# The last product of the MLP as seven block products (Strassen), with float32 activations

## The chip, the cores and the metric

The kernel runs on one core of a Trainium2 chip. The metric is the device time of one execution in microseconds, as the median of several runs. A separate execution was taken by the hardware profiler; all views of the profile come from that one. Engines are named as in the profile: PE is TensorE, DVE is VectorE, ACT is ScalarE, POOL is GpSimd, SP is SyncE, which here issues the loads and stores.

## The reference

One layer of a streaming encoder on 512 positions of width 1024: four parallel token mixers, a cross-attention, and a gated MLP. All numbers are float32. The change touches the MLP only:

```python
hf = _rms_norm(x, norm_ffn_pre[l])                        # 512 x 1024
u = _dwconv_causal(hf @ w_up[l], ffn_dw[l]) + ffn_dw_b[l] # w_up 1024 x 5632, conv of width 3
u_g, u_v = jnp.split(u, 2, axis=-1)                       # two halves of 2816
yff = (jax.nn.silu(u_g) * u_v) @ w_down[l]                # w_down 2816 x 1024
x = x + _rms_norm(yff, norm_ffn_post[l])                  # the output
```

## The kernel before

Every large product is formed in a split form: each float32 operand x is held as a high part hi (a cast by ACT to the format float32r) and a low part lo = x - hi (a subtraction by DVE, which reads x and hi and rounds to float32r). A product is then three matmuls, hi·hi, hi·lo and lo·hi, into the same PSUM bank (`mm3`). A matmul has a stationary operand of 128x128 and a moving one of 128x512.

`run_blocks` takes a stream of jobs, one for each block of weights, and writes out three jobs ahead: the load (SP), the cast (ACT) and the subtraction (DVE) of a block are written three blocks before the matmuls that use it. A scheduler then orders the instructions of each engine when the program is built, by a cost model; each engine works through its own queue in that order. Weights land in tiles `wr` (two buffers) and are split into `wh` and `wl`, four buffers each.

The MLP has two stages. `up_jobs` forms 44 blocks of the up-projection (24 matmuls each). The two blocks of a row group j (0 to 21) pass the convolution (one ACT operation and two of DVE from PSUM each), the gate (a tanh and two DVE operations, L1291 and L1292), and then `split` (ACT L152, DVE L153) writes the activations of j into `acth` and `actl`, which hold all 22 groups of 128 rows for all 512 positions.

`down_jobs` has 22 jobs, one for each group of 128 rows of `w_down`, with [128, 1024] weights each. For each, the 4 groups of 128 positions and the 2 halves of the output columns give 8 accumulators, which are the 8 banks of PSUM (tags mm, av, sc, tr, two each): 8 x 3 matmuls for a job, 528 in all. The last four jobs are held back, so that the accumulators end one after the other, and each group of positions is normed (square on ACT, L1345; root on POOL, L261 and L264; products and sums on DVE, L1348 and L1355) and stored while PE goes on with the next one.

Of the kernel before, what the change touches and what calls it, by code (L numbers as in the profile page):

```python
# [16 lines left out]
F32 = mybir.dt.float32  # L17
F32R = mybir.dt.float32r
AF = mybir.ActivationFunctionType
ALU = mybir.AluOpType  # L20
# [4 lines left out]
P = 128  # L25
S = 512
D = 1024
NT = S // P
# [5 lines left out]
NF = DFF // P  # L34
EPS = 1e-6
WB = 2 * 520
# [46 lines left out]
def hybrid_layer(ctx: ExitStack, tc: tile.TileContext, a: dict, out: bass.AP):  # L83
    nc = tc.nc
    V, A, G, PE, SP = nc.vector, nc.scalar, nc.gpsimd, nc.tensor, nc.sync


    gp = ctx.enter_context(tc.tile_pool(name="g", bufs=1))
# [7 lines left out]
    def bank(tag=None):  # L96
        if tag is None:
            turn_of.n += 1
            tag = "av" if turn_of.shared and turn_of.n % 2 else "mm"
        return psum.tile([P, 512], F32, tag=tag, name=f"ps_{tag}", bufs=2)  # L100
# [7 lines left out]
    w_up, w_down = a["w_up"][0], a["w_down"][0]  # L108
# [19 lines left out]
    for i in range(8):  # L128
        n = ("wh", "wl")[i % 2]
# [3 lines left out]
        elif i < 6:  # L133
            n = ("fz_raw", "fz", "fe", "fu", "fd")[i - 1]
# [7 lines left out]
    def weights_tile(kind):  # L142

        i = w_used[kind]
        w_used[kind] += 1
        return w_tiles.pop((kind, i), None) or gp.tile([P, WB], F32R, tag=f"{kind}{i % 4}", name=kind)


    def split(ps, hi, lo, scale=None):

        if scale is None:
            A.copy(hi, ps)  # L152
            V.tensor_tensor(lo, ps, hi.bitcast(F32), ALU.subtract)  # L153
        else:
            A.activation(hi, ps, AF.Copy if isinstance(scale, float) else AF.Identity, scale=scale)
            V.scalar_tensor_tensor(lo, ps, scale, hi.bitcast(F32), ALU.mult, ALU.subtract)
# [39 lines left out]
    def run_blocks(jobs, ahead=3):  # L196


        jobs = iter(jobs)
        pending = []  # L200

        def fetch():
            while True:
                job = next(jobs, None)
                if job is None:
                    return
                if job[1] is None:
                    pending.append((job[0] or (), job[2]))
                else:
                    pending.append((load_weights(*job[:2], *job[3:]), job[2]))  # L210
                if job[0] is not None:
                    return

        for _ in range(ahead):
            fetch()
        while pending:
            if pending[0][0]:
                fetch()
            w, body = pending.pop(0)
            body(*w)  # L220
            bg.tick()
# [9 lines left out]
    def mm3(ps, w_hi, w_lo, x_hi, x_lo, first, last):  # L231

        matmul(ps, w_hi, x_hi, first, False)
        matmul(ps, w_hi, x_lo, False, False)
        matmul(ps, w_lo, x_hi, False, last)
# [20 lines left out]
    def rstd_of(pool, parts, n=1):  # L256

        m = pool.tile([P, n], F32, tag="st_m", name="st_m", bufs=4)
        r = pool.tile([P, n], F32, tag="st_r", name="st_r", bufs=4)
        if len(parts) == 2:  # L260
            G.tensor_scalar(m, parts[0], parts[1], EPS, ALU.add, ALU.add)  # L261
        else:
            G.tensor_scalar(m, parts[0], EPS, None, ALU.add)
        G.tensor_tensor(r, m, nhalf[:, :n], ALU.pow)  # L264
        return r
# [21 lines left out]
    def new_ht():  # L287
        if ht_tiles:
            return ht_tiles.pop(0), ht_tiles.pop(0)
        return (gp.tile([P, NK, S], F32R, tag="hth", name="hth"),  # L290
                gp.tile([P, NK, S], F32R, tag="htl", name="htl"))
# [67 lines left out]
    for i, plan in enumerate(plans):  # L359
        r_t = m1p.tile([P, P], F32, tag="fbias" if i == 2 else "ck", name=f"rows{i}", bufs=2)  # L360
        n = 0
# [906 lines left out]
    def open_ffn():  # L1268
        bg.drain("n1")
        close(ns.work_)  # L1270
        close(ns.xp_)
        close(ns.xm_)
        ns.fp_, ns.fp = new_pool("ffn", False)
        ns.work = ns.fp
        ns.act = (ns.fp.tile([P, NF, S], F32R, name="acth"), ns.fp.tile([P, NF, S], F32R, name="actl"))
        ns.post = ns.fp.tile([P, D], F32, name="g_ffn")
        G.dma_start(ns.post, a["norm_ffn_post"][0].partition_broadcast(P))

    def up_jobs():
        st, held = {}, []  # L1280

        def done(j, i, ps):
            if i == 0:
                st[j] = ns.fp.tile([P, 2, S], F32, tag="c", name="c", bufs=2)
            c, ch = st[j], i * NF + j
            A.activation(c[:, i], ps, AF.Identity, bias=pc("fb", ch), scale=pc("fdw2", ch))
            taps(c[:, i], ps, lambda k: pc("fdw01", k * 44 + ch), 3)
            if i == 1:
                th = ns.fp.tile([P, S], F32, tag="th", name="th")
                A.activation(th, c[:, 0], AF.Tanh, scale=0.5)  # L1290
                V.scalar_tensor_tensor(th, th, 1.0, c[:, 0], ALU.add, ALU.mult)  # L1291
                V.scalar_tensor_tensor(c[:, 1], th, 0.5, c[:, 1], ALU.mult, ALU.mult)  # L1292
                split(c[:, 1], ns.act[0][:, j], ns.act[1][:, j])


        for n in range(2 * NF):
            def body(hi, lo, n=n):
                j, i = divmod(n, 2)
                if n > 3:
                    ps = bank()  # L1300
                    channel_major(ps, (hi, lo), ns.hf)
                    done(j, i, ps)
                    return
                if n == 0:
                    bg.drain("n0")
                ps = bank(("mm", "sc")[n % 2])
                (channel_major if n else by_pass)(ps, (hi, lo), ns.hf, slice(0, S // 2))
                held.append((j, i, ps, (hi, lo)))
                if n == 3:
                    open_ffn()  # L1310
                    for j, i, ps, w in held:
                        (channel_major if i or j else by_pass)(ps, w, ns.hf, slice(S // 2, S))
                        done(j, i, ps)
            yield *cols(w_up, n % 2 * DFF + n // 2 * P), body, V, same, HALF_SHIFT if n < 4 else 0

    def down_jobs():
        tail = 4
        held, ps = [], []

        def step(t, i, kk, hi, lo):  # L1320
            sl, csl = slice(t * P, (t + 1) * P), slice(i * 512, (i + 1) * 512)
            mm3(ps[t][i], ns.act[0][:, kk, sl], ns.act[1][:, kk, sl], hi[:, csl], lo[:, csl], kk == 0, kk == NF - 1)

        for kk in range(NF):
            def body(hi, lo, kk=kk):
                if kk == 0:
                    tags = (("mm", "mm"), ("av", "av"), ("sc", "sc"), ("tr", "tr"))
                    ps.extend([bank(n) for n in pair] for pair in tags)
                if kk < NF - tail:
                    for t in range(NT):  # L1330
                        for i in range(2):
                            step(t, i, kk, hi, lo)
                    return
                held.append((kk, hi, lo))
                if kk < NF - 1:
                    return
                for t in range(NT):
                    res, o = ns.out[t], ns.fp.tile([P, 2, S], F32, tag="c", name="o", bufs=2)
                    ms = []
                    for i in range(2):  # L1340
                        for w in held:
                            step(t, i, *w)
                        ms.append(ns.fp.tile([P, 1], F32, tag=f"pm{i}", name=f"pm{i}", bufs=2))
                        junk = ns.fp.tile([P, S], F32, tag="th", name="junk")
                        A.activation(junk, ps[t][i], AF.Square, scale=1.0 / math.sqrt(D), accum_out=ms[i])  # L1345
                        if i == 1:
                            r = rstd_of(ns.fp, ms)
                        V.tensor_tensor(o[:, i], ps[t][i], ns.post[:, i * 512:(i + 1) * 512], ALU.mult)  # L1348
                    for i in range(2):
                        sl = slice(i * 512, (i + 1) * 512)  # L1350
                        parts = 2 if (t, i) == (NT - 1, 1) else 1
                        for q in range(parts):
                            n = 512 // parts
                            c, d = slice(q * n, (q + 1) * n), slice(sl.start + q * n, sl.start + (q + 1) * n)
                            V.scalar_tensor_tensor(o[:, i, c], o[:, i, c], r, res[:, d], ALU.mult, ALU.add)  # L1355
                            SP.dma_start(out[t * P:(t + 1) * P, d], o[:, i, c])
            yield w_down[kk * P:(kk + 1) * P, :], [P, D], body

    def all_jobs():
        yield from mixer_jobs()  # L1360
# [43 lines left out]
```

## Time and profile before

| | |
|---|---|
| runs | 1080.5, 1080.79, 1081.97 us; median 1080.79 us |
| profiled execution | 1081.09 us, of which the span of the profile is 1079.3 us |
| mean granted clock of TensorE | 0.998 |
| PE, weight loads, DVE, ACT, POOL busy | 99%, 84%, 64%, 43%, 10% of the span |
| down stage, first to last matmul | 953.0 to 1073.0 us |

The span runs from the first to the last instruction of the profiled core. The 1.8 us between it and the execution's time lie around the program. Busy shares are means over stages; a stage is read from a table of stretches, and single instructions from the timeline. A line number in the profile is that of the helper that issues the instruction, so groups are told apart by tile names as well.

### The profile page before, as it was taken

Reading aid. Unit: us, or ns where it says so; the run is one execution under the profiler, and the core shown is the slowest. Engines: PE = TensorE matmul, PEld = TensorE weight load, DVE = VectorE, ACT = ScalarE, POOL = GpSimd, SP = SyncE. Lnnn points to the kernel's source line nnn. Section 1 sums busy time; section 2 is a strip of 40 time slices with the busy share of each in tenths; the row PEclk is TensorE's granted clock in tenths of the full one; section 3 lists DMA queues with packets and bytes.
Section 4 is the critical chain, followed back from the end, with each engine's and each line's share of the span. In section 5 each row is a group of like instructions: output and inputs, shape, how many; then the busy total and the mean of one; then the engine's idle time right before and its main releaser. Section 6 shows DMA issues by size and latency. Waiting matters only on the chain.

```text
span 1079.3 us, 14199 instructions
## 1 busy us (share of the span) xinstructions
PE 1071.2 (99%) x5453; PEld 910.7 (84%) x5453; DVE 695.9 (64%) x1131; ACT 465.3 (43%) x785; POOL 104.0 (10%) x189
## 2 busy tenths in 40 slices
PE   9999999999999999999999999999999999999997
PEld 8888888888888988888888899998888888888886
DVE  7899996466666467857464486868666666642224
ACT  5322222467464364654443365645444444431112
POOL 4000001000101033323000120120000000000001
PEclk9999999999999999999999999999999999999999
DMA  6433433332222243233155343134333333333322
GB/s 203 116 98 91 90 107 95 93 98 78 59 81 78 69 127 98 81 96 117 59 176 180 113 146 92 57 99 118 97 98 98 98 98 98 98 98 97 98 78 78
DMA packets 145848, 109.29 MB, mean 101 GB/s; under 512 B 3647, under 2 KB 133292, under 8 KB 145781
## 3 DMA queue, kind: packets, MB, share of 16 engines
q1 hardware_dynamic: 143219, 99.85, 31.1%
q0 software_dynamic: 2560, 8.54, 2.7%
q8 instruction: 43, 0.70, 0.3%
q14 instruction: 24, 0.20, 0.1%
q10 hardware_dynamic: 2, 0.00, 0.0%
HBM read 106.27 MB, written 2.11 MB: 100 GB/s over the span
## 4 chain that ended last, share of the span: by engine, by line
PE 99%; ACT 0%; DVE 0%; POOLq 0%; issue 0%; DVEq 0%; POOL 0%; ACTq 0%
PE ps_mm L224 52%; PE ps_av L224 31%; PE ps_sc L224 8%; PE ps_tr L228 3%; PE ps_tr L224 3%; PE ps_mm L431 1%; PE ps_av L431 1%; PE ps_mm L373 0%; PE ps_sc L378 0%; DVE o L1355 0%; PE ps_tr L415 0%; POOLq L1400 0%; ACT junk L1345 0%; ACT hth L152 0%; ACT hth L421 0%
## 5 line engine op out<-in xcount | busy, mean ns | idle before, releaser
L184 DVE TENSOR_TENSOR wl<-wr,wh 128x1024 fp32r<-128x1024 f32 (+1 forms) x172 | 212.2, 1235 | 194.2 <-ACT wh L183 193.7
L183 ACT CAST wh<-wr 128x1024 fp32r<-128x1024 f32 (+1 forms) x172 | 180.1, 1049 | 318.4 <-PE ps_mm L224 127.8
L224 PE MATMUL ps_mm<-hth,wh 128*128 128x512 f32 (+1 forms) x616 | 231.4, 382 | 0.2 <-ACT hth L152 0.2
L224 PE MATMUL ps_mm<-hth,wl 128*128 128x512 f32 (+1 forms) x616 | 230.0, 380 | 0.0
L224 PE MATMUL ps_mm<-htl,wh 128*128 128x512 f32 (+1 forms) x616 | 229.9, 380 | 0.0
L224 PEld LDWEIGHTS ps_mm<-hth,wh 128*128 128x128 f32 x616 | 114.3, 188 | 21.1 <-ACT hth L152 0.5
L224 PEld LDWEIGHTS ps_mm<-hth,wl 128*128 128x128 f32 x616 | 114.0, 188 | 21.1
L224 PEld LDWEIGHTS ps_mm<-htl,wh 128*128 128x128 f32 x616 | 114.0, 188 | 20.4 <-DVE htl L153 0.2
L224 PE MATMUL ps_av<-hth,wh 128*128 128x512 f32 (+1 forms) x328 | 122.4, 373 | 0.0
L224 PE MATMUL ps_av<-htl,wh 128*128 128x512 f32 (+1 forms) x328 | 122.4, 373 | 0.0
L224 PE MATMUL ps_av<-hth,wl 128*128 128x512 f32 (+1 forms) x328 | 122.3, 373 | 0.0
L584 DVE SCALAR_TENSOR_TENSOR y<-y,par,y 128x499 f32<-128x499 f32 (+28 forms) x120 | 82.3, 729 | 0.2
L224 PEld LDWEIGHTS ps_av<-htl,wh 128*128 128x128 f32 x328 | 61.7, 188 | 10.9
L224 PEld LDWEIGHTS ps_av<-hth,wh 128*128 128x128 f32 x328 | 61.5, 188 | 10.9
L224 PEld LDWEIGHTS ps_av<-hth,wl 128*128 128x128 f32 x328 | 61.5, 188 | 10.8
L224 PE MATMUL ps_mm<-y,wh 128*128 128x512 f32 x192 | 61.2, 394 | 0.0
L261 POOL TENSOR_SCALAR st_m<-pm,pm 128x1 f32<-128x1 f32 x12 | 6.4, 533 | 435.6 <-ACT junk L1345 350.2
L224 PEld LDWEIGHTS ps_mm<-y,wh 128*128 128x128 f32 x192 | 35.4, 188 | 6.8
L152 ACT CAST acth<-c 128x512 fp32r<-128x512 f32 x22 | 13.7, 621 | 56.9 <-DVE c L1292 56.9
L224 PE MATMUL ps_mm<-y,wl 128*128 128x512 f32 x96 | 37.6, 392 | 0.0
L907 POOL TENSOR_SCALAR fbias<-ck,cq 128x128 f32<-128x128 f32 (+3 forms) x32 | 27.6, 868 | 68.0 <-DVE st L913 63.5
L518 DVE SCALAR_TENSOR_TENSOR c<-ps_mm,par,c 128x510 f32<-128x510 f32 (+1 forms) x44 | 32.8, 745 | 0.7
(379 smaller groups left out, 1901.4 us busy)
## 6 DMA issues: line engine op xcount, KB each, us to landing
wr<-in_w_up SPq DMA_DIRECT2D x44, 512.0 KB
wr<-in_w_in SPq DMA_DIRECT2D x38, 512.0 KB
wr<-in_w_gate SPq DMA_DIRECT2D x32, 512.0 KB
wr<-in_w_down SPq DMA_DIRECT2D x22, 512.0 KB
wr<-in_w_branch SPq DMA_DIRECT2D x16, 512.0 KB
wr<-in_w_out SPq DMA_DIRECT2D x8, 512.0 KB
xr<-in_w_xkv SPq DMA_DIRECT2D x8, 512.0 KB
wr<-in_w_in SPq DMA_DIRECT2D x4, 520.0 KB
```

The source lines that it names most:

```text
L152: A.copy(hi, ps)
L183: order(A.copy(hi, raw[:, :n]))
L184: low.tensor_tensor(lo, raw[:, :n], hi.bitcast(F32), ALU.subtract)
L224: PE.matmul(ps, lhs, rhs, start=start, stop=stop)
L228: PE.transpose(ps, x, ident[:n, :n])
L261: G.tensor_scalar(m, parts[0], parts[1], EPS, ALU.add, ALU.add)
L431: keep(PE.matmul(banks[c][:, :S // 2], w[p == 1][:, k, c * P:(c + 1) * P], ht[p == 2][:, i * 4 + k, :S // 2], start=(i, p, k) == (0, 0, 0) ...
L518: V.scalar_tensor_tensor(dst[:, s:], src[:, :S - s], w(k), dst[:, s:], ALU.mult, ALU.add)
L584: V.scalar_tensor_tensor(dst[:, s:], src[:, :S - s], pc("conv_dw", k * 4 + j), dst[:, s:], ALU.mult, ALU.add)
L907: G.tensor_scalar(bias[:, :w], ck[j][:, :w], -1.0, cq[:, qt, head:head + 1], ALU.mult, ALU.add)
```

## The change

The last product is an [512 x 2816] by [2816 x 1024] one. It is cut in 2 x 2 blocks on both sides: positions 0 to 255 and 256 to 511, rows of `w_down` in even and odd groups of 128 (11 pairs), and columns 0 to 511 and 512 to 1023. Instead of the eight block products, seven are formed of sums and differences of the blocks (the variant with 15 sums), each as three matmuls as before: 7 products x 2 groups of 128 positions x 11 pairs x 3.

In the up stage the activations are no longer split. The last DVE operation of the gate writes them as float32 into tiles `qa` (4 blocks of 256 positions for each pair) and `qb` (3 blocks); for each pair POOL then forms four sums of 128x256 (`activation_sums`).

The down stage has two phases over the 11 pairs, with two jobs for each pair. Phase 0 forms M1, M6 (job 0) and M5, M7 (job 1) in all 8 banks; phase 1 forms M2, M3 (job 0) and M4 (job 1) in 6 of them. For a pair, phase 0 loads 768 KB of `w_down` into a tile `dw` (three buffers); POOL forms three sums of 128x512; ACT and DVE split four weight blocks of 512 columns and the four activation blocks (1024 columns in all). Phase 1 loads 512 KB again; POOL forms one sum; ACT and DVE split three weight blocks of 512 and three activation blocks (768 columns). The split activations lie in four slots, made of the two tiles (`hth`, `htl`) that held the input of the up stage; the split weights lie in the old four `wh` and `wl`. Between the phases (`middle`) DVE adds up M1, M6, M5 and M7. At the end (`ends`) the last three pairs of phase 1 are held back, and M4, M3 and M2 are added to what the middle left, normed and stored.

The core of the diff (the loops that end the result are cut, and so is the code that is taken out):

```diff
-        ns.act = (ns.fp.tile([P, NF, S], F32R, name="acth"), ns.fp.tile([P, NF, S], F32R, name="actl"))
+        ns.quart = [(ns.fp.tile([P, 4, S // 2], F32, tag=f"qa{q}", name="qa"),
+                     ns.fp.tile([P, 3, S // 2], F32, tag=f"qb{q}", name="qb")) for q in range(NF // 2)]
...
-                V.scalar_tensor_tensor(c[:, 1], th, 0.5, c[:, 1], ALU.mult, ALU.mult)
-                split(c[:, 1], ns.act[0][:, j], ns.act[1][:, j])
+                x = ns.quart[j // 2]
+                V.scalar_tensor_tensor(x[j % 2][:, 0:2].rearrange("p a b -> p (a b)"), th, 0.5, c[:, 1],
+                                       ALU.mult, ALU.mult)
+                if j % 2:
+                    activation_sums(*x)
...
+    def activation_sums(x, z):
+        G.tensor_tensor(x[:, 2], x[:, 1], z[:, 1], ALU.add)
+        G.tensor_tensor(x[:, 3], x[:, 0], x[:, 1], ALU.subtract)
+        G.tensor_tensor(x[:, 1], x[:, 2], x[:, 0], ALU.subtract)
+        G.tensor_tensor(z[:, 2], z[:, 0], x[:, 1], ALU.subtract)
...
+        pairs, hold, half = NF // 2, 3, S
+        order = [(phase, q) for phase in range(2) for q in range(pairs)]
...
+        def load(n):
+            while len(raws) < min(n, len(order)):
+                phase, q = order[len(raws)]
+                raw = ns.fp.tile([P, 3 * half], F32, tag="dw", name="dw", bufs=3)
+                rows = slice((2 * q + phase) * P, (2 * q + phase + 1) * P)
+                SP.dma_start(raw[:, :D], w_down[rows, :])
+                if phase == 0:
+                    SP.dma_start(raw[:, D:], w_down[(2 * q + 1) * P:(2 * q + 2) * P, half:])
+                raws.append(raw)
+
+        def split_to(hi, lo, x):
+            A.copy(hi, x)
+            V.tensor_tensor(lo, x, hi.bitcast(F32), ALU.subtract)
+
+        def activations(phase, q):
...
+                slot = parts["slots"][(phase * pairs + q - 1) % 4]
...
+            split_to(hi, lo, ns.quart[q][phase].rearrange("p a b -> p (a b)"))
...
+        def weights(phase, q, job):
+            if job == 0:
+                load(phase * pairs + q + 3)
+                activations(phase, q)
+            raw = raws[phase * pairs + q]
+            b = [raw[:, i * half:(i + 1) * half] for i in range(3)]
+            if (phase, job) == (1, 1):
+                G.tensor_tensor(b[2], b[0], t2.pop(q), ALU.subtract)
...
+                split_to(*both, b[2])
+                return [both],
+            hi, lo = weights_tile("wh"), weights_tile("wl")
+            both = [(hi[:, i * half:(i + 1) * half], lo[:, i * half:(i + 1) * half]) for i in range(2)]
+            if (phase, job) == (0, 0):
+                G.tensor_tensor(b[2], b[2], b[1], ALU.subtract)
+                t2[q] = ns.fp.tile([P, D], F32, tag=f"qa{q}", name="t2")[:, :half]
+                G.tensor_tensor(t2[q], b[2], b[0], ALU.add)
+                G.tensor_tensor(b[1], b[1], b[0], ALU.subtract)
+                split_to(*both[0], b[0])
+                split_to(*both[1], t2[q])
+            else:
+                split_to(hi[:, :D], lo[:, :D], raw[:, :D] if phase else raw[:, half:])
+            return both,
+
+        work = {(0, 0): (("M1", 0), ("M6", 1)), (0, 1): (("M5", 2), ("M7", 3)),
+                (1, 0): (("M2", 0), ("M3", 2)), (1, 1): (("M4", 1),)}
+
+        def step(name, t, q, a, w, phase):
+            hi, lo = parts[phase, q]
+            sl = slice(t * P, (t + 1) * P)
+            mm3(banks[name][t], hi[:, a, sl], lo[:, a, sl], *w, q == 0, q == pairs - 1)
...
+        def middle(job):
+            if job == 0:
...
+                for t in range(2):
+                    A.copy(parts["m1"][:, t], banks["M1"][t])
+                for t in range(2):
+                    V.tensor_tensor(u[:, t], parts["m1"][:, t], banks["M6"][t], ALU.add)
+                return
...
+            for t in range(2):
+                V.tensor_tensor(z7[:, t], u[:, t], banks["M7"][t], ALU.add)
+                V.tensor_tensor(u[:, t], u[:, t], banks["M5"][t], ALU.add)
+            for t in range(2):
+                V.tensor_tensor(z[:, t], u[:, t], banks["M7"][t], ALU.add)
+            for t in range(2):
+                ms[2 + t, 1] = square(z[:, t], 1)
+                V.tensor_tensor(z[:, t], z[:, t], ns.post[:, gains[1]], ALU.mult)
...
+        def ends():
...
+            def whole(name, t, x):
+                for q, job, ws in held:
+                    for (n, a), w in zip(work[1, job], ws):
+                        if n == name:
+                            step(name, t, q, a, w, 1)
+                V.tensor_tensor(x, x, banks[name][t], ALU.add)
+                return x
```

In `run_blocks`, a job may now bring its own function for the loads and splits, which is called where the load stood. Up to the first matmul of the down stage PE has the same instructions in the same order as before.

More of the change, by code (lines that the diff above doesn't have):

```diff
@@ L207, in fetch @@
                 if job[1] is None:
-                    pending.append((job[0] or (), job[2]))
+                    pending.append((job[0]() if callable(job[0]) else job[0] or (), job[2]))
                 else:
@@ L1314, in up_jobs @@
             yield *cols(w_up, n % 2 * DFF + n // 2 * P), body, V, same, HALF_SHIFT if n < 4 else 0
-    def down_jobs():
[L1317 to L1357, printed above, removed]
```

76 lines of the change are left out of this document (added).

## The prediction

> **What bounds the kernel now.** I read the page first, then the chain that ended last, then a table of stretches for the up and the down stage.
>
> ```profile
> span 1079.3 us, 14199 instructions
> ...
> PE 1071.2 (99%) x5453; PEld 910.7 (84%) x5453; DVE 695.9 (64%) x1131; ACT 465.3 (43%) x785; POOL 104.0 (10%) x189
> ...
> 855.42 5.44 PE ps_mm L224 x24
> ...
> 843.90:953.00 109.10, 109.10 (x483) 90.33 (x482) 73.67 (x91) 47.09 (x60) 0.00 (x0) 1.00 0.33 98
> 953.00:1073.00 120.00, 120.00 (x530) 99.05 (x528) 35.05 (x36) 26.05 (x35) 2.59 (x6) 1.00 0.28 88
> ```
>
> PE is busy all the time and is the chain. The third line, of that chain, gives the pitch: 24 matmuls in 5.44 us, 0.2267 us each. The last line is the down stage (PE, weight loads, DVE, ACT, POOL, granted clock, DMA share, GB/s): 528 x 0.2267 = 119.7 us of 120.0. DVE works there for 35 us, ACT for 26, POOL for 3. Matmuls taken out are time won, as long as the helpers that feed PE keep up; the question is whether three almost idle engines can take what is put on them.
>
> **What is removed.** 7 products x 2 position groups x 11 pairs x 3 = 462 matmuls in place of 528. The ordered queues of the two programs agree (5380 rows on PE for 5446). 66 x 0.2267 = 15.0 us less. PE alone would need 24 x 11 x 0.2267 = 59.8 us for phase 0 (5.44 a pair), and 18 x 11 x 0.2267 = 44.9 us for phase 1 (4.08 a pair).
>
> **What is added, on each engine.** The nearest rows:
>
> ```profile
> L184 DVE TENSOR_TENSOR wl<-wr,wh 128x1024 fp32r<-128x1024 f32 x60 | 73.5, 1224 | 110.9 <-ACT wh L183 110.9
> L183 ACT CAST wh<-wr 128x1024 fp32r<-128x1024 f32 x60 | 62.9, 1049 | 102.5 <-PE ps_tr L224 71.2 <-PE ps_av L224 22.2 <-PE ps_mm L224 7.5
> ...
> L153 DVE TENSOR_TENSOR actl<-c,acth 128x512 fp32r<-128x512 f32 x22 | 15.2, 691 | 13.7 <-ACT acth L152 13.7
> L152 ACT CAST acth<-c 128x512 fp32r<-128x512 f32 x22 | 13.7, 621 | 56.9 <-DVE c L1292 56.9
> ...
> L404 POOL TENSOR_TENSOR wa<-e,wa 128x512 fp32r<-128x512 f32 x4 | 5.1, 1320 | 2.1 <-ACT wa L401 2.1
> ...
> 11.23 3.85 POOL L404 TENSOR_TENSOR wa<-e,wa 128x512 fp32r<-128x512 f32 x3 [1.77 <-ACT wa L401]
> ...
> 954.23 1.22 DVE L184 TENSOR_TENSOR wl<-wr,wh 128x1024 fp32r<-128x1024 f32 x1 [1.32 <-ACT wh L183]
> 955.37 1.52 DVE L518 SCALAR_TENSOR_TENSOR c<-ps_av,par,c 128x510 f32<-128x510 f32 x2
> 10.00 1.35 DVE L424 TENSOR_TENSOR htl<-ps_tr,hth 128x512 fp32r<-128x512 f32 x2
> ```
>
> For a pair of phase 0, ACT casts 2 x 0.62 + 2 x 1.05 = 3.3 us, DVE subtracts 2 x 0.69 + 2 x 1.22 = 3.8 us, and POOL forms three sums, 3 x 1.28 = 3.9 us (1.28 is 3.85/3). Each by itself fits under 5.44 us. Behind one another DVE's instructions begin 1.14 us apart for 1024 columns (954.23 to 955.37) and end 0.66 us apart for 512 (1.35 less 0.69).
>
> They do not run beside each other, though. Four places of the timeline show it:
>
> ```profile
> 403.60 0.73 POOL L907 TENSOR_SCALAR fbias<-ck,cq 128x512 f32<-128x512 f32 x1 [1.71 <-DVE st L913]
> ...
> 405.06 1.22 DVE L184 TENSOR_TENSOR wl<-wr,wh 128x1024 fp32r<-128x1024 f32 x1
> 405.27 1.57 POOL L907 TENSOR_SCALAR fbias<-ck,cq 128x512 f32<-128x512 f32 x1
> ...
> 13.72 1.35 POOL L404 TENSOR_TENSOR wa<-e,wa 128x512 fp32r<-128x512 f32 x1
> 14.14 3.14 DVE L184 TENSOR_TENSOR wl<-wr,wh 128x1024 fp32r<-128x1024 f32 x2 [0.26 <-ACT wh L183]
> ...
> 488.58 0.48 POOL L907 TENSOR_SCALAR fbias<-ck,cq 128x256 f32<-128x256 f32 x1 [16.68 <-DVE st L913]
> ...
> 491.31 1.21 DVE L184 TENSOR_TENSOR wl<-wr,wh 128x1024 fp32r<-128x1024 f32 x1
> 491.49 1.91 POOL L907 TENSOR_SCALAR fbias<-ck,cq 128x256 f32<-128x256 f32 x1 [2.05 <-DVE st L913]
> 492.44 0.68 DVE L961 TENSOR_TENSOR acc<-acc,ge 128x512 f32<-128x512 f32 x1
> ```
>
> The POOL operation that takes 0.73 us at 403.60 takes 1.57 beside a DVE subtraction, and ends 0.56 us after it (406.84 against 406.28): it had waited. The two DVE subtractions at 14.14 take 3.14 us where two take 1.14 + 1.22 = 2.36: they wait for POOL's sum, which ends at 15.07. At 491.49 a POOL operation of 0.48 us takes 1.91, because a second DVE operation with both inputs in SBUF follows the first directly: POOL gets in only where DVE pauses. So a DVE instruction with two SBUF inputs and a POOL instruction that reads SBUF exclude each other. All splits and all sums of the new down stage are of these two kinds.
>
> [...] By engines alone the sum would be the 15.0 us less and the longer end; by the lock it is the following.
>
> A waiting POOL instruction does 0.73 - 0.56 = 0.17 us of its work ahead, so a sum holds the lock for 1.28 - 0.17 = 1.11 to 1.28 us. A pair of phase 0 then needs, one after the other, 2 x 1.14 + 2 x 0.66 + 3 x 1.11 = 6.9 us to 3.8 + 3.9 = 7.7 us, for 5.44 us of PE.
>
> **Phase 0 as a sum.** At the end of the up stage the splits of pair 0 and two sums each of pairs 0 to 3 are done, and the third of pair 0; more can't be, with three `dw`, `wh` and `wl` for two pairs, and slots that the up stage still reads. After it, by the ordered queues, DVE has 20 instructions of 1024 columns, 20 of 512 (one of them of the last gate), and of phase 1, which are queued in between, two of 768 and one of 512; POOL has 24 sums of 512, three of 256, and one of phase 1. Low: 20 x 1.14 + 20 x 0.66 + 2.5 + 24 x 1.11 + 1.7 + 1.1 = 67.9; high: 24.4 + 13.8 + 2.6 + 30.7 + 1.9 + 1.3 = 74.7 (768 columns at 0.90 to 0.96, 256 at half a sum, both estimates from these rows). With the first cast (1.05) ahead, the last split comes after 69.0 to 75.8 us, where PE wants it at 59.8 - 12 x 0.2267 = 57.1. Late by 11.9 to 18.7 us. I take 16: the engines hand over through ACT (sum, cast of 0.62, subtraction), which leaves the lock unused now and then, and where they alternate the whole records count.
>
> **Phase 1.** From there DVE has 10 x 512, 11 x 1024 and 9 x 768 columns of splits, 2 x 512 products in the middle, and 8 x 512 additions from PSUM; POOL has 10 sums. An addition from PSUM takes 0.69 us too (L1348, in the next rows). [...] Low: 6.6 + 12.5 + 8.1 + 1.3 + 5.3 + (11.1 - 5.3) = 39.6; high: 6.9 + 13.4 + 8.6 + 1.4 + 5.5 + 12.8 = 48.6. PE wants the last split after 12 + 152 matmuls, 37.2 us. Late by a further 2.4 to 11.4; I take 7, since the queue puts the middle's 7 us of DVE work ahead of the splits, and a bank's copy by ACT stands behind a cast that waits for POOL.
>
> **The end.** It follows PE at once:
>
> ```profile
> 1072.63 0.39 PE L224 MATMUL ps_tr<-wh,actl 128*128 128x512 f32 x1
> ...
> 1073.11 0.60 ACT L1345 ACTIVATE junk<-ps_tr 128x512 f32<-128x512 f32 x1 [2.01 <-PE ps_tr L224]
> 1073.83 0.69 DVE L1348 TENSOR_TENSOR o<-ps_tr,g_ffn 128x512 f32<-128x512 f32 x1 [2.00 <-ACT junk L1345]
> 1073.90 0.30 POOL L261 TENSOR_SCALAR st_m<-pm,pm 128x1 f32<-128x1 f32 x1 [4.49 <-ACT junk L1345]
> 1074.88 1.54 DVE L1355 SCALAR_TENSOR_TENSOR o<-o,st_r,res 128x512 f32<-128x512 f32 x3 [0.36 <-POOL st_r L264]
> ```
>
> Now an addition of 0.69 us stands before the square, and the results of the group before share DVE: 0.7 to 1.5 us more, 1.0 taken.
>
> **What costs nothing.** The up stage loses its splits of activations (0.62 on ACT, 0.69 on DVE for each group j) and gains POOL's sums of 256 columns, 4 for each 21.8 us; DVE is busy for 73.67 of 109.1 us there, so the lock has room, and PE keeps its order. 2.3 MB of `w_down` are moved in SP's queue ahead of the seventh block of up weights. That block is cast at 734.79 and its matmuls start at 746.62, as these rows show, so 10 us of cover stand against transfers of 512 KB that land in 4.0 to 5.9 us (the last two rows); 0, at most 3 if it is gone.
>
> ```profile
> 734.79 1.05 ACT L183 CAST wh<-wr 128x1024 fp32r<-128x1024 f32 x1 [0.35 <-DMA wr<-in_w_up]
> 746.62 5.44 PE ps_mm L224 x24
> ...
> g_ffn<-in_norm_ffn_post POOLq DMA_DIRECT2D x1, 512.0 KB, 4.0
> g_mem<-in_norm_mem POOLq DMA_DIRECT2D x1, 512.0 KB, 5.9
> ```
>
> **The sum.** -15.0 + 16 + 7 + 1 = +9 us, with ends -15.0 + 11.9 + 2.4 + 0.7 = 0 and -15.0 + 18.7 + 11.4 + 1.5 + 3 = +20. Made against the profiled execution's 1081.1 us, 1.8 us of it around the span and 0.3 above the median, that is 1090.
>
> **The rivals.** (1) The sums hide, and it is faster: DVE waits for ACT's casts anyway, and POOL's sums fall into these pauses. 1081.1 - 15.0 + 1 = 1067 if all fall there, and about 1079 if half of the 23 us of lateness stays. It decides from the point where a sum holds the lock for less than (5.44 - 3.6)/3 = 0.6 us. For it: DVE and POOL alone are at 3.8 and 3.9 us of 5.44. Against it: the row of 3.14 us, where a sum of just this shape kept DVE out till its end. Chance 0.16.
>
> (2) The hand-over becomes the bound: ACT works in order, a cast of a late sum blocks all casts behind it, and nothing overlaps. A pair then takes 3.9 + 3.8 + 0.62 + 1.05 = 9.4 us; nine pairs are late by 9 x 4.0 = 36, phase 1 by 11: 1081.1 - 15.0 + 36 + 11 + 1 = 1114. Against it: the casts of activations and of plain weights wait for no sum. Chance 0.12.
>
> (3) The change doesn't take the matmuls out, or PE's order changes ahead of it: excluded by the queues, no chance.
>
> **How the numbers follow.** The forecast of a slower kernel by the lock has 0.72, between 1081 and 1101; about 2.2 us, 0.2%, is what a measurement here can tell from no change. Its low end gives 0.05 to no change, and the high end of rival 1 another 0.01. Faster: 0.16 - 0.01 = 0.15. Slower: 0.72 - 0.05 + 0.12 = 0.79. The range of 1073 to 1104 leaves out most of rivals 1 and 2, some 0.2 together.
>
> **What would show it.** Right: matmuls in the down stage stall for DVE's low parts and ACT's casts of sums; the DVE subtractions there have records over 1.5 us and POOL's sums over 1.6; pairs of phase 0 come 7 us apart in place of 5.44; PE's busy share of the stage falls to about 80%. Wrong: pairs 5.44 us apart (rival 1), or over 9 (rival 2); or PE stalls in the up stage for weights, which would be the moved loads.

## The result and the profile after

| | before | after |
|---|---|---|
| median | 1080.79 us | 1086.4 us (5 runs, 1085.89 to 1090.12) |
| ratio | | 1.0056, 95% interval 1.0038 to 1.0074 |
| profiled execution | 1081.09 us, span 1079.3 | 1090.12 us, span 1088.3 |
| down stage, first to last matmul | 119.8 us (953.2 to 1073.0) | 122.7 us (956.7 to 1079.4) |
| end of the last matmul to the end of the span | 6.3 us | 8.9 us |

The changed kernel is slower by 0.56%, 5.6 us. A line of the page after, the largest wait of PE in the down stage, and a table of stretches by phase (PE, weight loads, DVE, ACT, POOL, granted clock, DMA share, GB/s):

```profile
PE 1064.4 (98%) x5387; PEld 899.5 (83%) x5387; DVE 767.8 (71%) x1178; ACT 490.1 (45%) x820; POOL 217.4 (20%) x277
...
PE ps_mm L225 <- DVE wl L1353: 6.5, 5, 2.5
...
956.00:1029.00 73.00, 65.30 (x268) 50.28 (x266) 68.97 (x48) 37.02 (x48) 52.88 (x30) 0.98 0.27 98
1029.00:1079.40 50.40, 46.69 (x198) 36.70 (x198) 45.61 (x51) 25.35 (x42) 14.72 (x13) 1.00 0.29 105
```

66 matmuls are gone, and PE, which was busy through the whole stage before, now waits for DVE's low parts. In phase 0 DVE is busy 69 of 73 us and POOL 53, with only 48 and 30 instructions: their records are long. The groups of the down stage:

```profile
L1353 DVE TENSOR_TENSOR wl<-dw,wh 128x1024 fp32r<-128x1024 f32 x21 | 34.4, 1642 | 2.8 <-ACT wh L1352 2.8
L1392 POOL TENSOR_TENSOR t<-dw 128x512 f32<-128x512 f32 x10 | 19.2, 1925 | 9.0 <-DVE htl L1353 6.3 <-DVE hth L1353 2.3
...
L1353 DVE TENSOR_TENSOR wl<-t,wh 128x512 fp32r<-128x512 f32 x10 | 14.9, 1492 | 0.0
L1393 POOL TENSOR_TENSOR dw<-dw 128x512 f32<-128x512 f32 x8 | 14.5, 1815 | 0.1
```

A DVE subtraction of 1024 columns takes 1.64 us in place of 1.22, one of 512 columns 1.49 in place of 0.69, a sum on POOL 1.8 to 1.9 in place of 1.28. One pair of phase 0 on the timeline shows how the two engines share the time:

```profile
1004.57 1.45 POOL L1390 TENSOR_TENSOR dw<-dw 128x512 f32<-128x512 f32 x1 [1.38 <-DMA dw<-in_w_down]
1004.80 4.00 DVE L1353 TENSOR_TENSOR wl<-dw,wh 128x1024 fp32r<-128x1024 f32 x2
...
1006.10 2.15 POOL L1392 TENSOR_TENSOR t<-dw 128x512 f32<-128x512 f32 x1
1008.21 1.74 POOL L1393 TENSOR_TENSOR dw<-dw 128x512 f32<-128x512 f32 x1
...
1008.72 1.78 DVE L1353 TENSOR_TENSOR wl<-t,wh 128x512 fp32r<-128x512 f32 x1
...
1010.42 1.21 DVE L1353 TENSOR_TENSOR hth<-qa,hth 128x1024 fp32r<-128x1024 f32 x1
1011.45 1.32 POOL L1390 TENSOR_TENSOR dw<-dw 128x512 f32<-128x512 f32 x1 [1.51 <-DMA dw<-in_w_down]
1011.56 4.00 DVE L1353 TENSOR_TENSOR wl<-dw,wh 128x1024 fp32r<-128x1024 f32 x2
...
1000.39 0.50 PE L225 MATMUL ps_mm<-wl,hth 128*128 128x512 f32 x1 [1.27 <-DVE wl L1353]
1007.16 0.50 PE L225 MATMUL ps_mm<-wl,htl 128*128 128x512 f32 x1 [1.02 <-DVE wl L1353]
1013.92 0.50 PE L225 MATMUL ps_mm<-wl,htl 128*128 128x512 f32 x1 [0.98 <-DVE wl L1353]
...
1029.13 0.50 PE L225 MATMUL ps_sc<-wh,htl 128*128 128x512 f32 x1 [0.48 <-ACT wr L1428]
```

PE starts the same place of successive pairs at 1000.39, 1007.16 and 1013.92: 6.76 us apart, where 24 matmuls need 5.44. DVE's two subtractions at 1004.80 (1024 and 512 columns) take 4.00 us in place of 1.8 (1.14 + 0.68), because a sum of POOL is let in ahead of each: POOL's sums end at 1006.02 and 1008.25. DVE's operations that follow one another directly begin 1.14 us apart for 1024 columns (the prediction's row) and 0.60 for 512 (rows with all sums on DVE, below), and a waiting sum was put at 1.11. One after the other, the pair's two DVE operations of 1024 columns, two of 512 and three sums make 2 x 1.14 + 2 x 0.60 + 3 x 1.11 = 6.81 us (the expectations below have 6.75, with 1.12 and 0.59). That is the pitch to 0.05 us, with nothing left over. The last line is the first matmul of phase 1, which waits for ACT's copy out of a bank.

The profiled execution holds 3.5 us that belong elsewhere, in a mixer whose instructions are the same in both kernels:

```profile
396.26 0.37 POOL L908 TENSOR_SCALAR fbias<-ck,cq 128x128 f32<-128x128 f32 x1 [3.33 <-DMA ck<-crows]
...
397.38 0.51 PE L225 MATMUL ps_sc<-qk 128*128 128x256 f32 x2 [1.50 <-DVE st L914]
...
400.00:405.00 5.00, 5.00 (x20) 4.12 (x19) 3.74 (x10) 3.95 (x9) 2.66 (x4) 0.73 0.38 105
```

POOL's operation waits for a transfer and begins 2.0 us later than before (394.28), PE waits, and the granted clock falls to 0.73; the down stage begins at 956.7 in place of 953.2. The other four runs lie at 1085.9 to 1087.0 us, so the account is made against the median of 1086.4.

### The profile page after: what moved, and what is told of

Read it like the earlier page. It is cut to its first block, busy times and chain, and to the rows that moved or that the text cites. A ratio compares the mean times of both kernels' runs of the same rounds, so it can differ in the third digit from the quotient of the medians.

```text
span 1088.3 us, 14306 instructions
## 1 busy us (share of the span) xinstructions
PE 1064.4 (98%) x5387; PEld 899.5 (83%) x5387; DVE 767.8 (71%) x1178; ACT 490.1 (45%) x820; POOL 217.4 (20%) x277
## 5 line engine op out<-in xcount | busy, mean ns | idle before, releaser
L183 ACT CAST wh<-wr 128x1024 fp32r<-128x1024 f32 (+1 forms) x150 | 157.0, 1049 | 294.4 <-PE ps_mm L225 183.1
L184 DVE TENSOR_TENSOR wl<-wr,wh 128x1024 fp32r<-128x1024 f32 (+1 forms) x150 | 188.3, 1257 | 138.3 <-ACT wh L183 137.8
L225 PEld LDWEIGHTS ps_av<-htl,wh 128*128 128x128 f32 x328 | 61.7, 188 | 10.7
L1353 DVE TENSOR_TENSOR wl<-dw,wh 128x1024 fp32r<-128x1024 f32 (+1 forms) x33 | 50.0, 1525 | 6.2 <-ACT wh L1352 6.1
L1352 ACT CAST wh<-dw 128x1024 fp32r<-128x1024 f32 (+1 forms) x33 | 29.8, 905 | 22.1 <-PE ps_mm L225 7.4
L152 ACT CAST pth<-ps_tr 128x512 fp32r<-128x512 f32 (+3 forms) x56 | 23.6, 449 | 22.9 <-PE ps_tr L229 22.7
```

What stands on the lines that cost most here:

```text
L183: order(A.copy(hi, raw[:, :n]))
L184: low.tensor_tensor(lo, raw[:, :n], hi.bitcast(F32), ALU.subtract)
L225: PE.matmul(ps, lhs, rhs, start=start, stop=stop)
L1352: A.copy(hi, x)
L1353: V.tensor_tensor(lo, x, hi.bitcast(F32), ALU.subtract)
```

## The experiments

The theory is that of the prediction: POOL's sums and DVE's subtractions, all with their inputs in SBUF, exclude each other (1.57 us for 0.73 and 3.14 for 2.36 in its rows); "the lock" is its word for this exclusion, and 1.11 us its estimate of what a waiting sum takes of it, from those rows. The rival is its rival 2, weakened: the hand-over sum, cast, subtraction, with ACT's queue in order, sets the pace. A second rival is the loads: POOL's first sum of a pair also waits for its transfer (1.38 and 1.51 us in the rows above). For each kernel the stage is cut at the first matmul of phase 0, the first of M2, and the end of the last one (from the timeline); "tail" is from there to the end of the span.

| kernel | phase 0 | phase 1 | tail | median, us | ratio to before |
|---|---|---|---|---|---|
| PE alone (0.2267 us a matmul) | 59.8 | 44.9 | | | |
| after | 72.5 | 50.3 | 8.9 | 1086.4 | 1.0056 |
| fills for sums | 60.0 | 45.1 | 8.9 | 1068.68 | 0.9893 |
| one more sum a pair | 79.0 | 48.8 | 8.9 | 1093.04 | 1.0101 |
| one operand | 61.3 | 45.1 | 8.4 | 1069.82 | 0.9897 |
| all sums on DVE | 60.5 | 45.1 | 12.0 | 1072.29 | 0.9918 |
| same, early ones on POOL, tail apart | 60.4 | 45.1 | 11.9 | 1072.54 | 0.9918 |
| phase 0's sums on DVE | 60.8 | 49.9 | 8.9 | 1075.49 | 0.9944 |
| same, tail apart | 60.8 | 49.3 | 8.2 | 1074.11 | 0.9931 |
| and 4 sums of phase 1 | 60.5 | 46.7 | 9.3 | 1071.04 | 0.9911 |
| and 6 sums of phase 1 | 60.5 | 45.7 | 10.2 | 1071.82 | 0.9914 |

The expectations below give the changed kernel 71.6 and 50.9 us; cut at the first matmul of M2 (1029.13), as all others are here, it has 72.5 and 50.3.

**Fills in place of sums.** A fill writes a constant and reads nothing; the sums are left out.

```diff
-                G.tensor_tensor(b[2], b[2], b[1], ALU.subtract)
+                for _ in range(2):
+                    G.memset(b[2], 0.5)
```

and so for the other three.

> Each sum of two weight blocks that GpSimd formed in the last stage is replaced by two fills of the same region (the sums are left out; every tile, hand-over, transfer and matmul stays). A fill only writes; by its rows elsewhere in the trace it takes about 0.53 us, two of them 1.06 against 1.11 for a sum alone. Theory 1 (VectorE's operations with two operands from SBUF and GpSimd's sums take turns at the same access, so that a pair of output blocks in phase 0 costs 2 x 0.59 + 2 x 1.12 + 3 x 1.11 = 6.75 us against 5.44 of matmuls): the fills do not take a turn, the pairs come down to 5.44 us, and phase 0 falls from 71.6 to about 60-62 us; time 1068 to 1073. Rival (the chain in which a sum goes from GpSimd through ScalarE's high part and VectorE's low part, with ScalarE's queue in order, sets the pace): the chain keeps its links, pairs stay at 6.4 us or more; time 1083 to 1087.

Measured: 1068.68 us, ratio 0.9893 (0.9871 to 0.9914). The groups and the two phases of that kernel:

```profile
L1353 DVE TENSOR_TENSOR wl<-t,wh 128x512 fp32r<-128x512 f32 x10 | 7.0, 696 | 0.8 <-ACT wh L1352 0.8
...
L1393 POOL MEMSET dw<- 128x512 f32 x14 | 7.4, 530 | 0.1
L1398 POOL MEMSET dw<- 128x512 f32 x14 | 7.4, 530 | 9.6 <-DMA dw<-in_w_down 9.2
...
953.00:1013.00 60.00, 60.00 (x266) 49.55 (x265) 48.88 (x55) 40.80 (x55) 32.61 (x62) 1.00 0.40 136
1013.00:1058.00 45.00, 44.85 (x198) 36.74 (x196) 33.48 (x45) 21.92 (x35) 8.85 (x16) 1.00 0.28 94
```

POOL is occupied for as long as with the sums (2 x 0.53 us measured, against 1.11 estimated), every hand-over from POOL to ACT and DVE is in place, and PE does not wait at all. The same subtraction takes 0.70 us in place of 1.49. What POOL does matters, not for how long: the rival falls. The loads fall as well in phase 0: the first fill of a pair waits for its transfer too (9.2 us in all, the line of L1398), and that costs PE nothing. In phase 1 the sum waits for a load and the fill does not; the kernel with one operand, below, keeps that wait, and its phase 1 is 45.1 us as well.

**One more sum on POOL.**

```diff
+                G.tensor_tensor(t2s[:, half:D], b[0], b[0], ALU.add)
```

> One more sum of two weight blocks on GpSimd per pair of phase 0, into the unused half of tile t, read by nobody. GpSimd's own work per pair goes from 3 to 4 sums of 1.11 us, 4.4 us against 5.44 of matmuls and 6.76 of the present pace, so that it has room for it if it works alone. Theory 1 (VectorE's operations with two operands from SBUF and GpSimd's sums take turns at one access, which is never unused in phase 0): every added sum of the stage, 8 or 9 of them, costs its whole 1.11 us; pairs 7.9 us apart, phase 0 longer by 9 to 10 us; time 1094 to 1097. Rival (the chain GpSimd, ScalarE, VectorE of a hand-over sets the pace): the added sum lies in GpSimd's idle time; time 1086 to 1088.

Measured: 1093.04 us, ratio 1.0101 (1.0081 to 1.0121): 6.6 us more than after, between the two expectations, nearer to the theory's. Its groups of phase 0 and its stretch:

```profile
L1395 POOL TENSOR_TENSOR t<-dw 128x512 f32<-128x512 f32 x10 | 18.1, 1805 | 0.0
...
956.00:1031.70 75.70, 64.51 (x252) 47.65 (x251) 72.91 (x47) 34.31 (x46) 70.92 (x39) 0.95 0.27 94
```

Phase 0 grew by 6.5 us (79.0 for 72.5), and by 7.0 without the 0.5 us that the changed kernel waits at its end. Of the ten added sums the first three stand in its first 13 us, where POOL had pauses in the changed kernel; the seven after that would make 7 x 1.11 = 7.8 us. The expectation counted eight or nine and so missed by the early ones. Phase 1 is 1.5 us shorter than after, which no run explains. POOL's idle time by itself (it was busy for 53 of 73 us, much of that waiting) gave the sums no room.

**One operand on DVE.**

```diff
-            V.tensor_tensor(lo, x, hi.bitcast(F32), ALU.subtract)
+            V.tensor_scalar(lo, hi.bitcast(F32), 0.5, None, ALU.mult)
```

> The low part in the last stage is formed as 0.5 times the high part (the subtraction is left out): VectorE reads one operand from SBUF instead of two, and still waits for ScalarE's high part; GpSimd's sums stay as they are. If only operations with two operands from SBUF take turns with GpSimd, the turns end: GpSimd's sums come down to 1.11 us, pairs to 5.44 us, time 1068 to 1073. If VectorE's operations with one operand take turns as well, pairs stay near 6.7 us and the time at 1083 to 1087. The rival of a chain through ScalarE gives 1083 to 1087 too, but with GpSimd's sums at 1.11 us.

Measured: 1069.82 us, ratio 0.9897 (0.9873 to 0.9921), so the time of the first reading, but not its records:

```profile
L1353 DVE TENSOR_SCALAR wl<-wh 128x512 fp32r<-128x512 f32 x19 | 20.3, 1111 | 0.0
L1392 POOL TENSOR_TENSOR t<-dw 128x512 f32<-128x512 f32 x10 | 15.8, 1579 | 5.4 <-ACT htl L1352 4.8
...
1022.82 0.42 DVE L1353 TENSOR_SCALAR n<-n 128x512 fp32r<-128x512 f32 x1
1023.15 0.69 DVE L1353 TENSOR_SCALAR wl<-wh 128x1024 fp32r<-128x1024 f32 x1
```

In its shortest records the one-operand operation takes 0.42 us for 512 columns and 0.69 for 1024, about half of the subtraction (0.69 and 1.22). Beside the sums of phase 0 those of 512 take 1.11 in the mean, and the sums take 1.58: the turns go on, each of DVE's only half as long. With begin-to-begin times of 0.33 (1022.82 to 1023.15) and about 0.60, a pair needs 2 x 0.33 + 2 x 0.60 + 3 x 1.11 = 5.2 us, just under 5.44. None of the three expectations had this. So this operation, with one input in SBUF, takes turns with POOL's sums as well: 1.11 us for 0.42.

**All sums on DVE.**

```diff
-                G.tensor_tensor(b[2], b[2], b[1], ALU.subtract)
+                V.tensor_tensor(b[2], b[2], b[1], ALU.subtract)
```

and so for the other three.

> The four kinds of weight sums of the last stage go from GpSimd to VectorE; nothing else is changed. Theory 1 (turns at one access): without GpSimd's sums nothing contends, and VectorE's own work per pair of phase 0 is 2 x 1.12 + 5 x 0.6 = 5.2 to 5.6 us against 5.44 of matmuls; phase 0 falls from 71.6 to 60-64 us, phase 1 from 50.9 to 46-48; time 1071 to 1076. Rival (VectorE's own queue or the hand-over through ScalarE sets the pace): VectorE has more to do than before and the pace is no better than 6.4 us a pair; time 1084 or more.

Measured: 1072.29 us, ratio 0.9918 (0.9901 to 0.9934), in the theory's range. A piece of its timeline, and its two phases:

```profile
993.08 0.68 DVE L1392 TENSOR_TENSOR t<-dw 128x512 f32<-128x512 f32 x1
993.68 0.68 DVE L1393 TENSOR_TENSOR dw<-dw 128x512 f32<-128x512 f32 x1
994.29 0.68 DVE L1390 TENSOR_TENSOR dw<-dw 128x512 f32<-128x512 f32 x1
994.89 0.68 DVE L1353 TENSOR_TENSOR wl<-dw,wh 128x512 fp32r<-128x512 f32 x1
...
953.00:1013.00 60.00, 59.93 (x263) 49.00 (x263) 59.15 (x76) 39.86 (x51) 5.53 (x3) 1.00 0.36 124
1013.00:1058.00 45.00, 45.00 (x199) 37.19 (x199) 38.60 (x53) 23.26 (x37) 1.76 (x3) 1.00 0.25 87
```

DVE has all the work now, 59 of 60 us in phase 0, and PE is fed all but without a gap in both phases. A sum costs DVE 0.60 us from begin to begin; on POOL it kept DVE out for 1.1 (4.00 us for 1.8 with two sums, at 1004.80 in the changed kernel). Of the 15 us of matmuls 14.3 are won (105.6 us in place of 119.8), and the tail, 12.0 us for 6.3 before, gives 5.7 back: the held-back products M4, M3 and M2 are formed in turns instead of one after the other, and DVE works without a pause for another 6.8 us behind the last matmul, on additions and norms. This run does not separate the order of the ends from DVE's backlog.

**Early sums left on POOL, products of the tail apart.** Of the second sum only the first pair's stays on POOL.

```diff
+                (G if q < 3 else V).tensor_tensor(b[2], b[2], b[1], ALU.subtract)
...
-                result(t, 1, x, x)
+                us.append(result(t, 1, whole("M3", t, u[:, t]), spare(2 + t))[1])
```

> As the kernel with the sums on VectorE, but the sums of the first three pairs, which are formed while the up product still runs, stay on GpSimd, and the products of the tail go to tiles of their own instead of in place, so that a product does not wait for ScalarE's square and the last addition does not stand behind it. Theory 1: phase 0 and phase 1 as in that kernel or 1 us shorter, and the tail 1 us shorter (8.9 to about 7.5); time 1070 to 1074. Rival (chain through ScalarE): 1083 or more, with the tail 1 us shorter.

Measured: 1072.54 us, ratio 0.9918 (0.9904 to 0.9933), no different from the kernel before it: phase 0 is as long (60.4 us for 60.5), and the tail is 11.9 us, not 7.5. The products end in the same order, DVE works for 6.8 us behind the last matmul again, and the place of the products makes no difference there.

**Phase 0's sums alone on DVE.** The last of the four sums (the one of phase 1) stays on POOL.

> Only the three sums of phase 0 go from GpSimd to VectorE; the one sum per pair of phase 1 stays on GpSimd. Theory 1: in phase 1 the turns add up to 1.12 + 0.59 + 0.87 on VectorE and 1.11 on GpSimd, 3.7 us per pair against 4.08 of matmuls, so that phase 1 can bear a sum on GpSimd once phase 0 does not hand it a backlog: no stall of TensorE in either phase, as with all sums on VectorE, and VectorE has 6.5 us less to do at the end, so that the additions and norms of the tail are not queued behind each other: tail 9 us instead of 12. Time 1068 to 1071. Rival (phase 1's late 6.0 us are its own, from GpSimd's sum and the hand-over): 1074 to 1077.

Measured: 1075.49 us, ratio 0.9944 (0.9926 to 0.9962): the rival's range, and the theory as I had put it missed. The tail is 8.9 as expected, but phase 1 takes 49.9 us. Waits of PE and the timeline of that kernel:

```profile
PE ps_sc L225 <- ACT htl L1352: 2.0, 1, 2.0
PE ps_sc L225 <- DVE htl L1353: 0.8, 1, 0.8
...
1025.15 1.29 POOL L1379 TENSOR_TENSOR dw<-dw,t 128x512 f32<-128x512 f32 x1 [4.09 <-DVE n L1353]
1025.65 1.88 DVE L1353 TENSOR_TENSOR wl<-dw,wh 128x1024 fp32r<-128x1024 f32 x1
1027.45 0.68 DVE L1438 TENSOR_TENSOR o<-o,ps_av 128x512 f32<-128x512 f32 x1
1027.48 1.30 POOL L1379 TENSOR_TENSOR dw<-dw,t 128x512 f32<-128x512 f32 x1 [1.04 <-DMA dw<-in_w_down]
1028.05 1.82 DVE L1353 TENSOR_TENSOR wl<-dw,wh 128x1024 fp32r<-128x1024 f32 x1
```

My sum of 3.7 us a pair left out the eight additions and two products of the step between the phases, which DVE does among the first pairs of phase 1. PE's two waits are 2.8 of the 5.0 us of lateness (49.9 for 44.9); after the first the granted clock is 0.56 to 0.58 from 1034 to 1038 us, so matmuls take longer there (7 in the 2 us from 1034, 11 in those from 1040, with the clock at 1.00). While DVE is behind with those additions, each sum on POOL costs it another 0.6 us (1.88 and 1.82 for 1.22). The addition from PSUM at 1027.45 is not held up: it takes 0.68 us, and the sum beside it 1.30.

**The same with the products of the tail apart.**

> As the kernel with phase 0's three sums on VectorE, and in the tail the products with the gain go to tiles of their own instead of in place. If the in-place product, which has to wait for ScalarE's square, is what holds back the last addition, the tail gets 0.6 to 1.0 us shorter: 1067.5 to 1070. If only the turns between VectorE and GpSimd's roots lengthen the tail, it stays as long: no difference.

Measured: 1074.11 us, ratio 0.9931 (0.9913 to 0.9949), against 0.9944 (0.9926 to 0.9962). The time is above the expected 1067.5 to 1070, which counted no stall in phase 1; with the granted clock at 1.00 from 1030 to 1042 us this time, PE waits 1.3 and 2.2 us there. The intervals overlap; in the profiled executions the tail is 8.2 us for 8.9. The order of the last matmuls is the same in both, so some 0.6 us of the tail hung on the in-place product; the medians can't show it by themselves.

**Four and six sums of phase 1 on DVE as well.**

```diff
-                G.tensor_tensor(b[2], b[0], t2.pop(q), ALU.subtract)
+                (V if q < 4 else G).tensor_tensor(b[2], b[0], t2.pop(q), ALU.subtract)
```

and with 6 for 4.

> The sums of phase 0 and those of the first 4 pairs of phase 1 on VectorE, the other 7 of phase 1 on GpSimd; the products of the tail in tiles of their own. With phase 1's sums all on GpSimd TensorE stalled for 3.0 and 3.8 us around pairs 2 to 4 of phase 1, where VectorE also had the eight additions, the two products and the squares' waits of the step between the phases; with all of them on VectorE it did not stall at all, but the tail was 12.0 us instead of 8.9 because the products ended in another order. Theory 1 (a sum on GpSimd takes 1.11 us of the shared access, on VectorE 0.60, which counts only while VectorE is behind): most of those stalls go, 0 to 1.5 us are left, tail 8.3: 1067.5 to 1070.5. Rival (the stalls come from the order of the additions, not from GpSimd's sums): 1073 to 1075.

> As the one before, with the sums of the first 6 pairs of phase 1 on VectorE and 5 on GpSimd. Here the last products of M4 and M3 end interleaved instead of one after the other, M2 still last. Theory 1: no stall of TensorE in either phase, last matmul as with all sums on VectorE, tail 8.0 to 9.5 us: 1067 to 1070. Rival: 1073 to 1075.

Measured: 1071.04 us, ratio 0.9911 (0.9896 to 0.9925), and 1071.82, ratio 0.9914 (0.9901 to 0.9927). PE's lateness in phase 1 falls from 4.4 us (49.3 less 44.9, with the same tail) to 1.8 and 0.8, so what it came from is POOL's sums while DVE is behind, not the order of the additions. Both times are 0.5 to 2 us over the expected ranges, mostly by tails of 9.3 and 10.2 us. With four sums moved the matmuls end in the same order as with none, yet DVE reaches its last addition late:

```profile
1060.91 0.68 DVE L1474 TENSOR_TENSOR wr<-wr,ps_sc 128x512 f32<-128x512 f32 x1
```

The last matmul ends at 1059.80, 1.1 us before. So DVE's backlog lengthens the tail even where the order is kept; with six sums moved M4 and M3 also end interleaved. These two and the kernel with all sums on DVE are faster than both kernels of this case by 0.8 to 0.9% and 1.3 to 1.4%, and can't be told from one another.

## Why the prediction was right, and where it was not

The forecast of a slower kernel by this exclusion held: 1086.4 us for 1090, inside the range. The fills (phase 0) and the kernel with all sums on DVE (both phases) show that PE's waits go when POOL's sums no longer take turns with DVE. Term by term, from the profiled executions, with the kernel with fills as the one that does not wait:

| term | predicted | measured |
|---|---|---|
| matmuls taken out | -15.0 | -14.7 (60.0 + 45.1 with fills, for 119.8) |
| phase 0 late | +16 (11.9 to 18.7) | +12.4 (72.5 for 60.0) |
| phase 1 late | +7 (2.4 to 11.4) | +5.2 (50.3 for 45.1) |
| tail | +1.0 (0.7 to 1.5) | +2.6 (8.9 for 6.3) |
| sum | +9 | +5.5; median 1086.4 less 1081.1 = +5.3 |

The misses partly cancel: the two phases were put 5.4 us too late, the tail 1.6 us too short.

**Phase 0** was mis-sized. It came near the low bound of 11.9, from begin-to-begin times and 1.11 us a sum; the 4 us on top were taken because the hand-over through ACT "leaves the lock unused now and then", and because "the whole records count" where the engines alternate. In the steady pairs neither counts: the sum of turns is 6.81 us and the pitch 6.76, and ACT's casts lie beside the other turns. The prediction's reading that "POOL gets in only where DVE pauses" doesn't hold there either: POOL and DVE take strict turns, one instruction each, though both have another ready, as the records at 1004.80 and 1006.10 show. So neither starves, and the cost is the plain sum of both engines' own times. At 491.49 in the kernel before, POOL did wait for two DVE operations in a row; no run shows what decides there. That the bound is met so closely is in part luck: its 0.66 us for 512 columns is read from an operation on PSUM, where splits in a row begin 0.60 apart; with 0.60 the bound is 10.7 us. Of the 12.4 us, 0.5 are the wait for ACT's copy at the switch; the other 1.2 are not broken down.

**Phase 1** came out inside its range and by the reasons given: the copy out of the bank, at 1029.13, and the step between the phases ahead of the splits. Its low end takes off 5.3 us of sums that run beside the additions from PSUM, and the 0 us at the low end of the whole forecast rests on that too; no run shows this 5.3 as such. What the runs showed is that single additions from PSUM do run beside a sum (0.68 and 1.30 us at 1027.45 with phase 0's sums on DVE), while the operation with one input, in SBUF, took turns (1.11 us for 0.42 in the kernel with one operand). With phase 0 cured it still lost 5.0 us there (49.9 for 44.9), and with four of its own sums moved to DVE as well 1.8.

**The tail** is beyond its bounds. The changed kernel's end:

```profile
1079.52 0.69 DVE L1448 TENSOR_TENSOR wr<-wr,g_ffn 128x512 f32<-128x512 f32 x1
...
1080.13 0.68 DVE L1470 TENSOR_TENSOR wr<-wr,ps_sc 128x512 f32<-128x512 f32 x1
...
1081.74 0.81 POOL L262 TENSOR_SCALAR st_m<-pm,pm 128x1 f32<-128x1 f32 x1 [0.72 <-ACT junk L1414]
1082.39 0.68 DVE L1448 TENSOR_TENSOR wr<-wr,g_ffn 128x512 f32<-128x512 f32 x1
1082.64 0.85 POOL L265 TENSOR_TENSOR st_r<-st_m,nhalf 128x1 f32<-128x1 f32 x1
```

The last matmul ends at 1079.41, but the addition begins at 1080.13, behind a product that had waited for the other group's square (0.6); the addition itself is 0.7; and POOL's two roots, one column each, take 0.81 and 0.85 us where they took 0.30 and 0.56 before (0.8 in all): DVE's operations beside them, at 1081.72 and 1082.39, have two SBUF operands, while beside the addition from PSUM a root of the other group still takes 0.56 (1080.46). The other 0.5 lie mostly in the results and stores behind. The prediction counted the addition and left out the exclusion at the one place where POOL stands on the path to the end.

**What costs nothing** held: PE does not wait for weights in the up stage, and in all other kernels, with the same moved loads, the down stage begins at 952.5 to 953.7, as before at 953.2. Of the signs, pairs at 6.76 us, subtractions at 1.49 to 1.64 and sums over 1.6 came as said, but PE's busy share of phase 0 is 89% (65.30 of 73.00) and not 80%, because phase 0 is less late and some matmuls ran at a granted clock of 0.50 (987 to 989 us, below).

**Rival 1** gave as its point a sum that holds the lock for under 0.6 us. With the sums on DVE a sum takes 0.60 us, a pair 2 x 1.14 + 5 x 0.60 = 5.28 us for 5.44 of matmuls, and PE just doesn't wait. That fits the point it gave; the changed kernel was on the other side of it because of the engine that formed the sums.

## What to carry to other kernels

An idle engine is free help only if it doesn't use what the busy one needs: here a sum on GpSimd cost VectorE 1.1 us, and on VectorE itself 0.60, so taking the help back turned 0.56% slower into 0.8 to 0.9% faster. Where two engines take turns, add up both engines' own times per step and hold the sum against the bound of the step; long records of a simple operation on both engines at once (here 1.49 us for 0.69 on VectorE, 1.8 to 1.9 for 1.28 on GpSimd) are the sign. Add up the steps that fall between two phases too, and look at each instruction behind the last matmul by itself.

## What the runs showed of the hardware

In the changed kernel a wait of PE of 2.53 us was followed by a granted clock of 0.50 for some microseconds (stretches as above):

```profile
985.76 0.50 PE L225 MATMUL ps_mm<-wl,htl 128*128 128x512 f32 x1 [2.53 <-DVE wl L1353]
...
987.00:989.00 2.00, 2.00 (x6) 1.54 (x5) 2.00 (x2) 1.21 (x3) 2.00 (x1) 0.50 0.94 359
989.00:991.00 2.00, 2.00 (x8) 1.60 (x8) 2.00 (x2) 1.57 (x2) 2.00 (x2) 0.79 0.06 22
991.00:993.00 2.00, 2.00 (x10) 1.35 (x8) 2.00 (x2) 1.05 (x1) 2.00 (x2) 1.00 0.12 12
```

The granted clock is 0.85 in the stretch from 985 us, 0.50 in that from 987, 0.79 in the next, and from 991 us, 5 us after the wait, 1.00 again. In the kernel with one more sum a pair, a wait just as long, 2.56 us, was followed by the full clock, so it is not the length of the wait alone that decides, and no run shows what does:

```profile
1054.31 0.73 PE L225 MATMUL ps_sc<-wh,htl 128*128 128x512 f32 x2 [2.56 <-DVE htl L1353]
...
1055.00:1057.00 2.00, 2.00 (x11) 1.64 (x10) 2.00 (x2) 0.09 (x1) 1.60 (x1) 1.00 0.00 0
```

In the changed kernel the lower clock cost little, since DVE's low parts set the pace at that place anyway: PE waits for one again at 993.62 (0.49 us).
